# Two layers of a hybrid trunk: mLSTM normaliser states moved as rows, adaLN paced evenly with buffers of its own

## The chip, the cores and the metric

The kernel runs on one core of a Trainium2 chip. The metric is the device time of one execution in microseconds (us), median of several runs.

## The reference

Two layers work on 128 context tokens and 512 latent tokens, 640 rows of 1024 channels, in float32. Each layer computes, for either token group with its own conditioning vector:

```python
sh1, sc1, gt1, sh2, sc2, gt2 = split(silu(cvec) @ w_mod[l] + b_mod[l], 6)     # adaLN
h = rmsnorm(x, g1) * (1 + sc1) + sh1
z = h @ w_in + b_in          # inputs of four mixers and their gates
x = x + gt1 * (sum_i sigmoid(gates_i) * (mixer_i(z) @ w_b[i])) @ w_o
h = rmsnorm(x, g2) * (1 + sc2) + sh2
x = x + gt2 * (silu(h @ w1a) * (h @ w1b)) @ w2
```

Mixer A is neighbourhood attention, B dense attention with few key heads, C windowed attention with a sink, D a bidirectional mLSTM with 4 heads of 128 channels. For each head and direction D carries a matrix C (128 x 128), a normaliser n (128) and a stabiliser m. The latent tokens start from cached states (`state_C`, `state_n`, `state_m`), and the final states of the context tokens are outputs (`ml_C`, `ml_n`, `ml_m`). At the end comes one more RMSNorm.

## The kernel before

**Work and tiling.** Tokens lie in five tiles of 128 (the fifth is the context). Every matrix product is made of three fp32r matmuls per slab, for a high and a low part of both factors (`mm3`, L391 to L393). Weights come by `wload`: a DMA of 512 KB into one of two raw buffers (L374), a ScalarE cast into the high part (L379) and a VectorE subtraction for the low part (L380), into rings of five. A projection by `fm` goes over two groups of columns (256 and 384 tokens), eight slabs each, and yields after the fourth slab and at the end of each group; `tm` does the same over the five token tiles.

**Order.** `mixers` writes the order out by hand. A list of bulk work (the projections of A, D, B, C and the merges M00 to M33, each with a rate) is run by `drive`. After each yield of bulk work it calls `tick()`, and takes as many steps from the attention and mLSTM streams as the rate gives credit for. Then `layer` does the output projection (four column blocks `n`), a norm (`norm_tm`), 22 FFN columns in four groups and the next norm, with `tick()` in every yield (`run`). A scheduler then sorts the instructions of each engine by priority and a simulated time; weight loads have a high priority. All DMAs are issued by SP, in order.

**adaLN.** The modulation of a layer has 12 chunks of 512 columns (two each for shift, scale and gate of either norm). Chunks 0 to 3 of layer 0 are made in `start`. All others are background work: `bg` holds generators, and `tick()` takes `bg[0]` steps of them per tick. One step (`adaln_acc`) takes one 128 x 512 slab of `w_mod`: for the latent vector VectorE multiplies and adds it into a sum (L456); for the context vector ScalarE multiplies (L450) and GpSimd adds (L452). After eight slabs `adaln_cols` transposes both sums on TensorE (L463, four transposes into an S and four into a T bank) and reduces them on VectorE (L464). Gate chunks are transposed back, get their bias from `b_mod` and go to DRAM (`gt_d`), from where `gate_rows` loads them. Six chunks of layer 0 are queued at the first merge of C (M20), at one step per tick, and the rest is forced (`bg_steps(1000)`) before the output projection; 10, 11 and all of layer 1 follow in the FFN at 0.8 per tick. Their buffers are taken from those that attention and merges use (`qs`, `ofs`, `ta`).

**mLSTM.** `d_rows` (L1272 to L1349) makes the decay rows of all heads, with DMAs through DRAM. `d_attn` then goes over the heads: `states` loads C and n of both directions into a P buffer (L1398, L1399), `final` stores the context's C and n (L1441, L1442) from `ta`, of which there is one. Each n is a column: 128 partitions of one float, so 128 pieces of 4 bytes.

Lines of the steps below: L1571 is the last work of the merge of branch C (i = 2) of each column block, L1754 the product in an FFN column, L1595 and L1596 the residual add, L623 the front of a norm.

Of the kernel before, what the change touches and what calls it, by code (L numbers as in the profile page):

```python
# [63 lines left out]
for _i in range(4):  # L64
    for _j in range(8):
# [5 lines left out]
                           + ([np.arange(O_MI, O_MI + 16)] if h == 0 else [])) for h in range(4)]  # L71

S_N1, S_N2, S_GQ, S_GK, S_MG, S_SINK, S_BM = NFM, NFM + 8, NFM + 16, NFM + 17, NFM + 18, NFM + 22, NFM + 30
NSM = NFM + 62
# [5 lines left out]
DEFER = 2  # L80
BGRATES = (1.0, 0.8)
BGFL, BGJ, W3 = 0, 2, 1
RATES = (0.9, 0.7, 1.1, 1.1)
# [135 lines left out]
def trunk(ctx: ExitStack, tc: tile.TileContext, a: dict, depth: int):  # L219
# [84 lines left out]


    small = arena("sa", {1: 16, 2: 16, 5: 4, 10: 4, 40: 2})
    ssq = arena("ss", {1: 16})
# [157 lines left out]

    def adaln_chunk(l, ch):
        gate = (ch // 2) % 3 == 2
        accs = [ofs.take() for _ in range(2)]
        slots = [(qs, qs.take()), (ofs, ofs.take()), (ofs, ofs.take())]
        bufs = [slots[0][1][:, 0:512], slots[0][1][:, 512:1024], slots[1][1][:, :512]]  # L470
        tmps = [slots[2][1][:, :512], ta512()]

        def load(k):
            if k < KT:
                SY.dma_start(bufs[k % 3], a["w_mod"][l, P * k:P * k + P, 512 * ch:512 * ch + 512])
            elif gate and k == KT:
                for v in range(2):
                    SY.dma_start(bufs[2][4 * v:4 * v + 4, :P],
                                 a["b_mod"][l, 512 * ch:512 * ch + 512].rearrange("(j n) -> j n", n=P))

        for k in range(2):
            load(k)
        yield True
        for k in range(KT):
            adaln_acc(accs, bufs[k % 3], k, tmps[k % 2])
            load(k + 2)
            yield True
        if gate:
            col = smallb(10)[:, :8]
            adaln_cols(lambda v: col[:, 4 * v:4 * v + 4], accs)  # L490
            yield True
            ps = acc()
            T.transpose(ps[:8, :P], col, ident)
            V.tensor_tensor(bufs[0][0:8, :P], ps[:8, :P], bufs[2][0:8, :P], ALU.add)
            for v in range(2):
                SY.dma_start(gt_d[l][ch // 6, v, 512 * (ch % 2):512 * (ch % 2) + 512].rearrange("(j n) -> j n", n=P),
                             bufs[0][4 * v:4 * v + 4, :P])
        else:
            adaln_cols(lambda v: mod_slice(ch)[:, :, v], accs)
        have.add((l, ch))  # L500
        ofs.give(*accs)
        for pl, t in slots:
            pl.give(t)
        yield True

# [3 lines left out]
    def start():  # L509
# [81 lines left out]
        bigs.give(big)  # L591
        ms.give(*xT)
        return first

# [199 lines left out]
    def a_proj(l, p, d, big=None, hook=None, first=None):  # L794
# [83 lines left out]
        if first:  # L878
            SY.dma_start(tab, a["rope"])
            SY.dma_start(cmask, a["cmask"])  # L880
            SY.dma_start(bone, a["bone"])

    def a_attn(l, d):
# [375 lines left out]
    def d_rows(l, d):  # L1259
# [4 lines left out]
        ws_ = held[1][:, :NTOK]  # L1264
        rows4 = [t[:, :1280].rearrange("p (w n) -> p w n", w=2) for t in held[2:4]]
        z = zif
        lf = small(40).rearrange("p (t c) -> p t c", t=NTT)
# [9 lines left out]
        for (t0, nt) in ((0, 4), (4, 1)):  # L1277
            ps = bT()
            for tt in range(nt):
                T.transpose(ps[:16, tt * P:(tt + 1) * P], z[:, t0 + tt, :], ident)  # L1280
            S.copy(t16[:16, t0 * P:(t0 + nt) * P], ps[:16, :nt * P])
        yield
        for dr in range(2):
# [94 lines left out]
    def d_attn(l, d):  # L1378
        need = {0: (0, 1, 2, 4), 1: (3, 2, 1, 4)}

        def head(h):
# [12 lines left out]
            def states():  # L1394

                CS = st["CS"] = [p640()[:, :516].rearrange("p (c x) -> p c x", c=4) for _ in range(2)]
                for dr, c in ((0, 0), (1, 3)):
                    SY.dma_start(CS[dr][:, c, :P], a["state_C"][l, dr, h])  # L1398
                    SY.dma_start(CS[dr][:, c, P:P + 1], a["state_n"][l, dr, h].rearrange("(p o) -> p o", o=1))  # L1399

# [34 lines left out]
            def final():  # L1435
                cf = ta512()
                for dr in range(2):
                    ps = bS()
                    T.matmul(ps[:, :129], st["kws"][dr][:, 3, :], va[:, 4, :], start=True, stop=True)
                    S.copy(cf[:, 256 * dr:256 * dr + 129], ps[:, :129])  # L1440
                    SY.dma_start(a["ml_C"][l, dr, h], cf[:, 256 * dr:256 * dr + 128])  # L1441
                    SY.dma_start(a["ml_n"][l, dr, h].rearrange("(p o) -> p o", o=1),  # L1442
                                 cf[:, 256 * dr + 128:256 * dr + 129])

# [54 lines left out]
        for h in range(4):  # L1499
# [39 lines left out]
            yield  # L1539
        yield  # L1540
        yield
        heads[3][8]()
# [35 lines left out]

    have = set()

    def gate_rows(l, w):

        assert {(l, 6 * w + 4), (l, 6 * w + 5)} <= have
        gts = [p640() for _ in range(4)]
# [72 lines left out]
    def mixers(l, d, *start):  # L1657
        done.clear()

        def mg(i, jj, needs=(), rate=0.0):  # L1660
            def gen():
                if i == 2 and jj == 0 and l == 0:
                    bg[0] = BGRATES[0]
                    bg[2] += [adaln_chunk(0, ch) for ch in range(4, 10)]
                yield from merge(l, i, jj, d, i == 0, i == 2)
            return f"M{i}{jj}", needs, rate, gen()
# [26 lines left out]
    def layer(l, *start):  # L1693
# [10 lines left out]
        for n in range(2):  # L1704
            if n == BGFL:
                bg_steps(1000)
            p = wo(n)
# [6 lines left out]
            residual_tm(xs, p, KT, mg_lhs, gts, n)  # L1714
        pieces = {2: wo(2), **pieces}
        hook = norm_tm(xs, pieces, KT, mg_lhs, gts, ms, 1)
        ms.give(*extra[0])
# [3 lines left out]
        if l + 1 < depth:  # L1721
            smalls(l + 1)
        bg[0] = 0.0
        if l == 0:
            bg[2] += [adaln_chunk(0, ch) for ch in (10, 11)]
        if l + 1 < depth:
            bg[2] += [adaln_chunk(l + 1, ch) for ch in range(12)]
        j0 = 0
        for g, cnt in enumerate(FF_SPLIT):
# [4 lines left out]
            for jx in range(cnt):  # L1734
# [6 lines left out]
                if g == 3 and jx == 2:  # L1741
                    pieces[3] = fo(3, bufs)
                if j == BGJ:
                    bg[0] = BGRATES[1]
                pl = ks if g % 2 == 0 else (ms if jx < 4 else qs)
# [21 lines left out]
            if g == 3:  # L1767
                bg_steps(1000)
                if l + 1 == depth:
                    fin.append(ks.take())  # L1770
# [13 lines left out]
            j0 += cnt  # L1784
        bg[0] = 0.0
        if l + 1 < depth:
# [19 lines left out]
def layouts(x_prompt, x_sample, cache_na_kv, cache_gqa_kv, cache_swa_kv, state_mlstm_C, state_mlstm_n, state_mlstm_m,  # L1806
# [17 lines left out]
    ins["w_mod"] = f(w_mod)  # L1824
    ins["b_mod"] = f(b_mod)
    ins["wflat"] = pack_weights(w_in, f(w_branch), f(w_out), f(w_ffn_in), f(w_ffn_out))
# [10 lines left out]
    for w in range(2):  # L1837
        for s in range(2):
            at = S_BM + 16 * w + 8 * s
            sm[:, :, at:at + 8] = bm[:, 3 * w + s].transpose(0, 2, 1)  # L1840
    ins["smalls"] = sm
    ins["gqa_k_g"] = f(gqa_k_g)
    ins["btm0"] = f(b_in[:, TM0_COLS])
# [18 lines left out]
def build(ins, L):  # L1862
    import concourse.bacc as bacc

    nc = bacc.Bacc("TRN2", target_bir_lowering=False, num_devices=1)
    a = {}
# [17 lines left out]
```

## Time and profile before

| | |
|---|---|
| median of 3 runs | 2850.89 us (2850.05 to 2851.22) |
| the profiled execution | 2846.38 us, span 2844.6 us |
| TensorE busy (matmuls) | 2741.0 us, 96% |
| VectorE, ScalarE, GpSimd busy | 1870.2, 1347.7, 531.1 us |
| mean granted TensorE clock | 0.988 |

Busy time is the time in which an engine runs an instruction. In the rows below PE is TensorE's matmuls, PEld its weight loads, DVE VectorE, ACT ScalarE, POOL GpSimd, SP the engine that issues DMAs. PEclk is the granted share of TensorE's full clock. A wait `A <- B` says that A's engine stood idle until B was done.

### The profile page before, as it was taken

The numbers are of one execution on the slowest core, as the hardware profiler recorded it, in microseconds if no ns is written. First come the engines' busy times: TensorE is split into PE (matmuls) and PEld (weight loads), VectorE is DVE, ScalarE is ACT, GpSimd is POOL, SyncE is SP. The second block draws the span as 40 slices with busy tenths as digits, with TensorE's granted clock in tenths as the row PEclk, the third lists the DMA queues.
The fourth block names the chain that finished last, engine by engine and source line by source line (L and its number), as shares of the span: only waits on it lengthen the run. The fifth ranks groups of instructions, "written<-read, shape, count | busy, mean of one in ns | idle before, by whom it ended". The sixth has DMA issues, their size and how long they took to land.

```text
span 2844.6 us, 51810 instructions
## 1 busy us (share of the span) xinstructions
PE 2741.0 (96%) x19942; PEld 2692.0 (95%) x19942; DVE 1870.2 (66%) x4392; ACT 1347.7 (47%) x3122; POOL 531.1 (19%) x474
## 2 busy tenths in 40 slices
PE   8999999999988898989999999999999999999998
PEld 5999999999988898989999999999999999999998
DVE  7776567878788769785456766577888435334344
ACT  6764345656553544443237753356566334222322
POOL 0000001101166337471120000011100121101011
PEclk9999999999999999999999999999999999999999
DMA  6223331111255245452222223321111232222231
GB/s 243 83 90 92 72 69 60 46 57 60 72 164 174 94 149 160 141 164 97 90 96 81 96 92 87 63 70 45 47 62 46 90 134 68 67 82 75 72 101 66
DMA packets 117736, 264.30 MB, mean 93 GB/s; under 512 B 17536, under 2 KB 43520, under 8 KB 117488
## 3 DMA queue, kind: packets, MB, share of 16 engines
q1 hardware_dynamic: 117488, 260.99, 29.4%
q8 instruction: 156, 2.56, 0.4%
q14 instruction: 92, 0.75, 0.1%
HBM read 252.74 MB, written 7.95 MB: 92 GB/s over the span
## 4 chain that ended last, share of the span: by engine, by line
PE 75%; DVE 7%; DMA 6%; ACT 4%; issue 4%; POOL 2%; SPq 0%; DVEq 0%; POOLq 0%; ACTq 0%
PE acc L392 21%; PE acc L391 21%; PE acc L393 21%; PE O L1197 2%; DMA q<-w_mod 2%; PE T L1187 2%; DVE of L456 2%; DMA raw<-wflat 2%; DVE wlo L380 1%; DMA of<-w_mod 1%; POOL of L452 1%; ACT whi L379 1%; PE S L1154 1%; PE S L1155 1%; PE T L923 1%
## 5 line engine op out<-in xcount | busy, mean ns | idle before, releaser
L391 PE MATMUL acc<-hT,whi 128*128 128x256 f32 (+1 forms) x3392 | 1057.4, 313 | 10.2 <-DVE hT L643 3.1
L392 PE MATMUL acc<-hT,whi 128*128 128x256 f32 (+1 forms) x3392 | 1056.1, 312 | 3.3 <-DVE hT L588 1.5
L393 PE MATMUL acc<-hT,wlo 128*128 128x256 f32 (+1 forms) x3392 | 1053.5, 311 | 1.3 <-DVE wlo L380 1.3
L380 DVE TENSOR_TENSOR wlo<-raw,whi 128x512 fp32r<-128x512 f32 (+1 forms) x632 | 482.6, 768 | 398.8 <-ACT whi L379 397.0
L379 ACT CAST whi<-raw 128x512 fp32r<-128x512 f32 (+1 forms) x632 | 387.9, 619 | 630.0 <-PE acc L392 373.0
L391 PEld LDWEIGHTS acc<-hT,whi 128*128 128x128 f32 x3392 | 642.5, 190 | 16.1 <-DVE hT L643 4.1
L392 PEld LDWEIGHTS acc<-hT,whi 128*128 128x128 f32 x3392 | 643.1, 190 | 6.8 <-DVE hT L644 2.2
L393 PEld LDWEIGHTS acc<-hT,wlo 128*128 128x128 f32 x3392 | 642.6, 190 | 3.0 <-DVE wlo L380 1.8
L1596 POOL TENSOR_TENSOR big<-big,t 128x256 f32<-128x256 f32 x150 | 127.4, 852 | 603.9 <-DVE t L1595 592.1
L1566 POOL TENSOR_TENSOR m<-m,f 128x256 f32<-128x256 f32 x96 | 100.5, 1050 | 568.1 <-DVE f L1564 315.0
L391 PE MATMUL acc<-whi,kv 128*128 128x256 f32 x660 | 185.0, 283 | 7.2 <-DVE t L1595 4.4
L392 PE MATMUL acc<-wlo,kv 128*128 128x256 f32 x660 | 184.6, 283 | 3.0 <-DVE wlo L380 3.0
L393 PE MATMUL acc<-whi,kv 128*128 128x256 f32 x660 | 184.3, 282 | 0.0
L703 ACT CAST pth<-T 128x512 fp32r<-128x512 f32 (+1 forms) x232 | 118.1, 521 | 100.7 <-PE T L1187 50.1
L391 PE MATMUL acc<-big,whi 128*128 128x256 f32 (+1 forms) x512 | 158.8, 311 | 2.7 <-ACT f L1558 2.7
L393 PE MATMUL acc<-big,wlo 128*128 128x256 f32 (+1 forms) x512 | 159.9, 312 | 0.2 <-DVE wlo L380 0.2
L392 PE MATMUL acc<-big,whi 128*128 128x256 f32 (+1 forms) x512 | 158.4, 310 | 0.0
L704 DVE TENSOR_TENSOR ptl<-T,pth 128x512 fp32r<-128x512 f32 (+1 forms) x232 | 137.2, 602 | 30.2 <-ACT pth L703 29.4
L1595 DVE TENSOR_TENSOR t<-acc,P 128x256 f32<-128x256 f32 x200 | 83.2, 420 | 109.5 <-PE acc L393 97.4
L452 POOL TENSOR_TENSOR of<-of,ta 128x512 f32<-128x512 f32 x80 | 126.1, 1577 | 114.7 <-ACT of L450 91.8
L391 PEld LDWEIGHTS acc<-whi,kv 128*128 128x128 f32 x660 | 125.0, 190 | 8.3 <-DVE t L1595 5.0
L392 PEld LDWEIGHTS acc<-wlo,kv 128*128 128x128 f32 x660 | 124.1, 189 | 3.8 <-DVE wlo L380 3.8
(392 smaller groups left out, 5560.1 us busy)
## 6 DMA issues: line engine op xcount, KB each, us to landing
raw<-wflat SPq DMA_DIRECT2D x308, 512.0 KB
q<-w_mod SPq DMA_DIRECT2D x126, 256.0 KB
of<-w_mod SPq DMA_DIRECT2D x40, 256.0 KB
kv<-nbias SPq DMA_DIRECT2D x16, 576.0 KB
raw<-wflat SPq DMA_DIRECT2D x24, 256.0 KB
kv<-mdr SPq DMA_DIRECT2D x16, 320.0 KB
big<-x_sample SPq DMA_DIRECT2D x8, 512.0 KB
P<-gt_d SPq DMA_DIRECT2D x32, 128.0 KB
```

The source lines that it names most:

```text
L379: S.copy(hi[:, :n], raw[:, s0:s0 + n])
L380: V.tensor_tensor(lo[:, :n], raw[:, s0:s0 + n], hi[:, :n].bitcast(F32), ALU.subtract)
L391: T.matmul(ps, lhs(k, 0), rhs(k, 0), start=(k == 0), stop=False)
L392: T.matmul(ps, lhs(k, 0), rhs(k, 1), start=False, stop=False)
L393: T.matmul(ps, lhs(k, 1), rhs(k, 0), start=False, stop=(k == kn - 1))
L452: G.tensor_tensor(accs[v][:, :512], accs[v][:, :512], tmp, ALU.add)
L456: V.scalar_tensor_tensor(accs[v][:, :512], w, s, accs[v][:, :512], ALU.mult, ALU.add)
L703: S.copy(hi[:, :n], ps[:, :n])
L704: V.tensor_tensor(lo[:, :n], ps[:, :n], hi[:, :n].bitcast(F32), ALU.subtract)
L1566: G.tensor_tensor(mt[:, c0:c0 + n], mt[:, c0:c0 + n], gate[:, c0:c0 + n], ALU.add)
L1595: V.tensor_tensor(t[:, :256], ps[:, :256], gt[:, 256 * v:256 * v + 256], ALU.mult)
L1596: (V if n == 3 else G).tensor_tensor(xs[tt][:, 256 * n:256 * n + 256], xs[tt][:, 256 * n:256 * n + 256], t[:, :256], ALU.add)
```

## The change

The column loads and stores of n become one load and one store of 8 rows of 128 floats per layer, with a TensorE transpose each and small column copies on GpSimd (`ncol`). The background adaLN becomes one generator over all 20 chunks, started at the end of `start` and stepped at 0.25 per tick throughout, with four slab buffers, a pair of sums and one temporary of its own; between the last slab and the transposes it has two empty steps. `bg_until` makes further steps where a chunk is wanted that isn't there yet. The gate's bias comes from a constant that is loaded once. The new buffers are allocated first, in 15 KB per partition that a smaller DMA descriptor memory sets free (`dynamic_dma_scratch_size` 1024), with a pad that leaves every other buffer at its address.

```diff
-BGRATES = (1.0, 0.8)
-BGFL, BGJ, W3 = 0, 2, 1
+BGRATE = 0.25
+W3 = 1
...
+    ncol = [cp.tile([P, 8], F32, name=f"ncol{i}") for i in range(2)]
+    wm_tiles = [cp.tile([P, 512], F32, name=f"wm{i}") for i in range(4)]
+    msum = [cp.tile([P, 512], F32, name=f"msum{v}") for v in range(2)]
+    mtmp = cp.tile([P, 512], F32, name="mtmp")
+    gcol = cp.tile([P, 8], F32, name="gcol")
+    grow = cp.tile([8, P], F32, name="grow")
+    bgate = cp.tile([P, depth, 2, KT], F32, name="bgate")
+    cp.tile([P, 72], F32, name="pad")
...
-    def adaln_chunk(l, ch):
...
+    def adaln_all(items):
+        def load(x):
+            if x < KT * len(items):
+                (l, ch), k = items[x // KT], x % KT
+                SY.dma_start(wm_tiles[x % 4], a["w_mod"][l, P * k:P * k + P, 512 * ch:512 * ch + 512])
+        load(0)
+        load(1)
+        for i, (l, ch) in enumerate(items):
+            for k in range(KT):
+                adaln_acc(msum, wm_tiles[(KT * i + k) % 4], k, mtmp)
+                load(KT * i + k + 2)
+                yield True
+            yield True
+            yield True
+            if (ch // 2) % 3 == 2:
+                adaln_cols(lambda v: gcol[:, 4 * v:4 * v + 4], msum)
...
+                yield True
+                ps = acc()
+                T.transpose(ps[:8, :P], gcol, ident)
+                V.tensor_copy(grow, ps[:8, :P])
...
+            else:
+                adaln_cols(lambda v: mod_slice(ch)[:, :, v], msum)
+            have.add((l, ch))
             yield True
...
+    def bg_until(l, *chs):
+        while not all((l, ch) in have for ch in chs):
+            assert bg[2]
+            bg_steps(1)
...
+        bg[0] = BGRATE
+        bg[2].append(adaln_all([(l, ch) for l in range(depth) for ch in range(0 if l else 4, 12)]))
         return first
...
+            SY.dma_start(bgate.rearrange("p l w k -> p (l w k)"), a["bgate"])
...
+        nrow = held[1][:8, NTOK:NTOK + P]
+        SY.dma_start(nrow, a["state_n"][l].rearrange("d h p -> (d h) p"))
...
+        ps = bT()
+        T.transpose(ps[:, :8], nrow, ident[:8, :8])
+        V.tensor_copy(ncol[0], ps[:, :8])
         yield
...
-                    SY.dma_start(CS[dr][:, c, P:P + 1], a["state_n"][l, dr, h].rearrange("(p o) -> p o", o=1))
+                    G.tensor_copy(CS[dr][:, c, P:P + 1], ncol[0][:, 4 * dr + h:4 * dr + h + 1])
...
-                    SY.dma_start(a["ml_n"][l, dr, h].rearrange("(p o) -> p o", o=1),
-                                 cf[:, 256 * dr + 128:256 * dr + 129])
+                    G.tensor_copy(ncol[1][:, 4 * dr + h:4 * dr + h + 1], cf[:, 256 * dr + 128:256 * dr + 129])
...
+        ps = bT()
+        T.transpose(ps[:8, :P], ncol[1], ident)
+        nout = ta512()[:8, :P]
+        V.tensor_copy(nout, ps[:8, :P])
+        SY.dma_start(a["ml_n"][l].rearrange("d h p -> (d h) p"), nout)
...
-        assert {(l, 6 * w + 4), (l, 6 * w + 5)} <= have
+        bg_until(l, 6 * w + 4, 6 * w + 5)
...
-            if n == BGFL:
-                bg_steps(1000)
...
+        bg_until(l, *range(6, 10))
...
-                if j == BGJ:
-                    bg[0] = BGRATES[1]
...
-                bg_steps(1000)
+                if l + 1 < depth:
+                    bg_until(l + 1, *range(4))
...
-    nc = bacc.Bacc("TRN2", target_bir_lowering=False, num_devices=1)
+    nc = bacc.Bacc("TRN2", target_bir_lowering=False, num_devices=1, dynamic_dma_scratch_size=DMA_RING)
```

## Rows read from the trace of the kernel before

**Rows 1.** The page, part 1: busy us of each engine, its share, instructions.

```profile
PE 2741.0 (96%) x19942; PEld 2692.0 (95%) x19942; DVE 1870.2 (66%) x4392; ACT 1347.7 (47%) x3122; POOL 531.1 (19%) x474
```

**Rows 2.** Lines L1571 and L1754 by stretch: duration ns, first and last start us.

```profile
L1571 ACT ACTIVATE kv<-m x6: 721/737/738, 795.7 to 861.4; 128x640 fp32r<-128x640 f32 x6
...
L1571 ACT ACTIVATE kv<-m x6: 738/740/741, 2241.6 to 2293.6; 128x640 fp32r<-128x640 f32 x6
...
L1754 DVE TENSOR_TENSOR f<-acc,f x22: 409/484/558, 1200.9 to 1451.7; 128x256 f32<-128x256 f32 x11, 128x384 f32<-128x384 f32 x11
...
L1754 DVE TENSOR_TENSOR f<-acc,f x20: 423/488/558, 2635.2 to 2806.6; 128x256 f32<-128x256 f32 x10, 128x384 f32<-128x384 f32 x10
```

**Rows 3.** Busy us by stage: length, PE, PEld, DVE, ACT, POOL, PEclk, DMA, GB/s.

```profile
795.70:1451.70 656.00, 601.98 (x4342) 589.88 (x4341) 462.90 (x635) 265.69 (x488) 295.82 (x221) 0.98 0.42 133
2241.60:2806.60 565.00, 564.58 (x4200) 563.82 (x4199) 228.31 (x418) 169.46 (x334) 73.23 (x84) 1.00 0.26 84
...
800.00:900.00 100.00, 88.48 (x598) 85.42 (x598) 81.29 (x93) 45.59 (x75) 62.33 (x46) 0.97 0.54 174
```

**Rows 4.** Waits of PE, 795 to 1310 us: us in total, times, longest.

```profile
PE S L463 <- DVE of L456: 17.9, 8, 3.6
PE T L463 <- POOL of L452: 6.8, 5, 2.3
```

**Rows 5.** The chain that ended last: start us, us, what.

```profile
286.61 10.98 DMA raw<-wflat
...
402.16 9.96 DMA raw<-wflat
...
1737.16 11.22 DMA raw<-wflat
...
1851.42 9.87 DMA raw<-wflat
```

**Rows 6.** Timeline of PE from 845.8 us: start us, us, what.

```profile
845.86 0.66 PE L463 MATMUL S<-ident,of 128*128 128x128 f32 x4
846.27 0.42 PE L392 MATMUL acc<-hT,whi 128*128 128x384 f32 x1
```

**Rows 7.** VectorE by form, 100 to 200 and 800 to 900 us; then line L456.

```profile
L380 DVE TENSOR_TENSOR wlo<-raw,whi 128x512 fp32r<-128x512 f32 x16 | 10.9, 688 | 4.4 <-ACT whi L379 4.4
...
L380 DVE TENSOR_TENSOR wlo<-raw,whi 128x512 fp32r<-128x512 f32 x21 | 24.3, 1166 | 2.7 <-ACT whi L379 2.7
...
L456 DVE SCALAR_TENSOR_TENSOR of<-kv,csil,of x12: 730/732/747, 18.5 to 30.5; 128x512 f32<-128x512 f32 x12
```

**Rows 8.** Lines L452 and L464: duration ns min/median/max, first and last start us.

```profile
L452 POOL TENSOR_TENSOR of<-of,ta x80: 1263/1619/2236, 783.2 to 1305.6; 128x512 f32<-128x512 f32 x80
...
L464 DVE TENSOR_REDUCE modr<-S x12: 674/681/692, 847.4 to 1259.9; 128x4 f32<-128x512 f32 x12
```

**Rows 9.** Busy us by stage: the mixers of layer 0.

```profile
60.00:785.00 725.00, 711.87 (x5212) 704.87 (x5211) 526.87 (x1534) 415.60 (x1040) 55.12 (x50) 0.99 0.25 71
```

**Rows 10.** Busy us by stage: the two fullest windows of VectorE in those mixers.

```profile
680.00:700.00 20.00, 20.00 (x147) 19.88 (x146) 19.63 (x53) 13.39 (x34) 2.15 (x2) 1.00 0.26 80
720.00:740.00 20.00, 20.00 (x148) 19.83 (x147) 19.00 (x54) 13.57 (x34) 2.07 (x2) 1.00 0.27 89
```

**Rows 11.** DMA, 275 to 305 us in 40 slices of 0.75 us.

```profile
GB/s 87 1 0 0 0 0 0 0 0 0 0 0 105 1 4 98 17 104 0 11 27 49 27 49 38 33 38 44 324 423 368 131 0 0 0 0 0 0 0 0
```

**Rows 12.** Timeline of SP, 270 to 305 us.

```profile
286.17 0.33 SPq L1442 DMA_DIRECT2D ml_n<-ta  x1
```

**Rows 13.** Busy us by stage: the four stretches with a late weight load.

```profile
286.00:302.00 16.00, 10.04 (x71) 9.65 (x70) 5.68 (x17) 4.26 (x12) 0.00 (x0) 0.79 0.55 84
...
400.00:416.00 16.00, 12.24 (x93) 11.95 (x93) 7.42 (x24) 7.24 (x27) 1.42 (x2) 0.96 0.63 76
...
1732.00:1752.00 20.00, 16.18 (x124) 15.86 (x123) 6.89 (x17) 6.73 (x17) 0.00 (x0) 0.93 0.40 70
...
1849.00:1866.00 17.00, 13.32 (x97) 13.04 (x96) 8.42 (x25) 7.49 (x27) 1.42 (x2) 0.88 0.58 73
```

More of the change, by code (lines that the diff above doesn't have):

```diff
@@ L71 @@
                            + ([np.arange(O_MI, O_MI + 16)] if h == 0 else [])) for h in range(4)]
+DMA_RING = 1024
 S_N1, S_N2, S_GQ, S_GK, S_MG, S_SINK, S_BM = NFM, NFM + 8, NFM + 16, NFM + 17, NFM + 18, NFM + 22, NFM + 30
@@ L464, in adaln_cols @@
             V.tensor_reduce(dst(v), ps.rearrange("p (j n) -> p j n", j=4), AX.X, ALU.add)
-    def adaln_chunk(l, ch):
[L467 to L476, printed above, removed]
-                for v in range(2):
[L478 to L486, printed above, removed]
-            yield True
[L488 to L504, printed above, removed]
@@ new lines, in trunk @@
+    have = set()
+    def adaln_all(items):
[14 more added lines that the diff above has]
+                adaln_cols(lambda v: gcol[:, 4 * v:4 * v + 4], msum)
+                w, h = ch // 6, ch % 2
+                for v in range(2):
+                    V.tensor_tensor(gcol[:, 4 * v:4 * v + 4], gcol[:, 4 * v:4 * v + 4], bgate[:, l, w, 4 * h:4 * h + 4],
+                                    ALU.add)
+                yield True
+                ps = acc()
+                T.transpose(ps[:8, :P], gcol, ident)
+                V.tensor_copy(grow, ps[:8, :P])
+                for v in range(2):
+                    SY.dma_start(gt_d[l][w, v, 512 * h:512 * h + 512].rearrange("(j n) -> j n", n=P), grow[4 * v:4 * v + 4])
+            else:
+                adaln_cols(lambda v: mod_slice(ch)[:, :, v], msum)
+            have.add((l, ch))
+            yield True
@@ L1577, in merge @@
             bigs.give(d["big"])
-    have = set()
     def gate_rows(l, w):
-        assert {(l, 6 * w + 4), (l, 6 * w + 5)} <= have
+        bg_until(l, 6 * w + 4, 6 * w + 5)
         gts = [p640() for _ in range(4)]
@@ L1661, in gen @@
             def gen():
-                if i == 2 and jj == 0 and l == 0:
-                    bg[0] = BGRATES[0]
-                    bg[2] += [adaln_chunk(0, ch) for ch in range(4, 10)]
                 yield from merge(l, i, jj, d, i == 0, i == 2)
@@ L1722, in layer @@
             smalls(l + 1)
[L1723 to L1727, printed above, removed]
         j0 = 0
@@ L1767, in layer @@
             if g == 3:
-                bg_steps(1000)
-                if l + 1 == depth:
+                if l + 1 < depth:
+                    bg_until(l + 1, *range(4))
+                else:
                     fin.append(ks.take())
@@ L1784, in layer @@
             j0 += cnt
-        bg[0] = 0.0
         if l + 1 < depth:
@@ L1824, in layouts @@
     ins["w_mod"] = f(w_mod)
-    ins["b_mod"] = f(b_mod)
     ins["wflat"] = pack_weights(w_in, f(w_branch), f(w_out), f(w_ffn_in), f(w_ffn_out))
@@ L1841, in layouts @@
     ins["smalls"] = sm
+    ins["bgate"] = np.ascontiguousarray(bm[:, 2::3].transpose(3, 0, 1, 2).reshape(P, L * 2 * KT))
     ins["gqa_k_g"] = f(gqa_k_g)
```

## The prediction

> **What bounds the kernel now.** I read the page first, to see which engine is full: TensorE is busy in 2741.0 of 2844.6 us [rows 1], so nothing but its 104 us of idle time, and time at a low clock, is there to be won. Next the windows by stage, to see where those us lie. The adaLN burst of the kernel before runs from the first merge of branch C in layer 0 into that layer's FFN. Layer 1 does the same merges, output projection and FFN without adaLN, so it measures what the burst costs. From the first L1571 to the last L1754 layer 0 takes 795.7 to 1451.7 = 656.0 us, layer 1 2241.6 to 2806.6 = 565.0 us [rows 2]: 91.0 us more. In layer 0 TensorE idles 656.0 - 602.0 = 54.0 us of it at a granted clock of 0.98, in layer 1 0.4 us at 1.00 [rows 3]. The waits of TensorE there, to see what came last: the adaLN transposes L463 waited 17.9 us for VectorE's accumulation and 6.8 us for GpSimd's [rows 4]; the rest are small waits of bulk matmuls for evictions and weight splits on a crowded VectorE. Last the chain of waits in the mixers, where four stretches are no TensorE work but a weight load of 9.9 to 11.2 us [rows 5].
>
> **Part one, adaLN paced at 0.25.** It removes the burst. What stays is TensorE's own work: 20 chunks x 8 transposes; four take 846.27 - 845.86 = 0.41 us of the queue [rows 6], so 160 take 16.4 us, wherever they stand, and the eight gate transposes under 1 us. Stalls that can go: 91.0 - 17 = 74 us. Check: 54 us idle, and 2% of 656 us is 13 us at a lower clock, 67 us; the other 7 are slower matmuls inside busy time.
>
> Where the work goes. A tick is one yield of bulk work. By the code a group of 8 slabs gives two ticks, a group of 4 one: in the mixers 4 x 12 (A) + 4 x 18 (D) + 10 + 16 (B) + 8 + 16 (C) + 16 x 12 (merges) = 362, after them 20 + 20 + 22 x 8 + 120 + 20 = 356, so 718 per layer. The new generator has 8 accumulating steps per chunk, two empty ones and one or two to finish, 11 or 12: 12 plain chunks x 11 + 8 gate chunks x 12 = 228 steps, 912 ticks. So 90 steps fall in layer 0's mixers, 89 in the stretch of the old burst, 49 in the first half of layer 1's mixers: 139 of 228 move beside attention, some 97 accumulations and 12 chunk ends. Deadlines are met far ahead: the gates of chunks 4 and 5 are 24 steps = 96 ticks, wanted at tick 362, so the new forced steps cost nothing. Empty steps put over 8 ticks between the last accumulation and its transposes, which covers L463's wait.
>
> What it costs there. On VectorE an accumulation takes 0.73 us by itself; and ops that read two SBUF tensors slow down beside GpSimd's add: L380 takes 0.688 us in a stretch without adds and 1.166 us in the burst [rows 7]. GpSimd was busy in 62 of those 100 us [rows 3], so a fully covered op takes about twice as long, and a 1.6 us add [rows 8] costs VectorE at most 0.8 us: 0.73 to 1.5 us per accumulation, I take 1.2; and 1.36 us of reduces per chunk [rows 8]. With 725 us for some 350 ticks, 20 us hold 2.4 steps, 1.7 accumulations: 2.0 + 0.3 = 2.3 us more VectorE work per 20 us. Layer 0's mixers have it 526.9 of 725.0 us busy [rows 9], so the sum fits, but two windows of 20 us stand at 19.63 and 19.00 us, with TensorE full all the same [rows 10]. They overflow by 1.9 and 1.3 us, and other windows have room. Bounds for the loss in the mixers: nothing (the windows after absorb it) to the 97 x 1.5 + 24 x 0.68 = 162 us of all this work on the path. Nearest is the row in which VectorE at 98% costs TensorE nothing, so I take the two overflows with as much again for the lower clock behind a stall, 6 us; 5 us for 24 reduces that now hold a score or transpose bank between attention blocks; and 4 us for the two row chains of the mLSTM (d_rows), of many small VectorE ops, that have adaLN ops among them. A gain is excluded, since the mixers only get work. In the stretch of the old burst, where layer 1 leaves VectorE over half free [rows 3], the steps are hidden; in the two norms, where GpSimd lies on the chain, I allow 7 us. Losses: 22 us, 0 to 162. The w_mod loads (256 KB every 12 us or so) are requested two steps, about 16 us, ahead; the 9.9 to 11.2 us of the slowest loads [rows 5] lie inside that. What is queued behind one that is late is all of VectorE. A weight load that stands behind one on SP lands later by 256 KB at some 400 GB/s [rows 11], 0.7 us, and has a second raw buffer as cover. ScalarE gets one multiplication per step and is busy for 415.6 of 725 us [rows 9]; GpSimd, at 55.1 of 725 us, lets a power for a head norm wait up to 1.6 us behind an add, which the 5 and 4 us hold. The gate bias joins a load at the start instead of 16 small ones; the pad and the smaller descriptor memory have no instruction: nothing.
>
> **Part two, the normaliser states as rows.** Removed are 16 loads and 16 stores of 128 single floats each. In the stretch of the first such pair of stores the DMA moves 11 to 49 GB/s in nine slices of 0.75 us, then 324 to 423 [rows 11]; the second store is issued at 286.17 us [rows 12], and the weight load behind it at 286.61 takes 10.98 us [rows 5]. The same stands behind the stores of the last head and again in layer 1. TensorE's idle time in those four stretches is 5.96 + 3.76 + 3.82 + 3.68 = 17.2 us, and granted clocks of 0.79, 0.96, 0.93 and 0.88 lose 3.4 + 0.6 + 1.4 + 2.0 = 7.4 us [rows 13]: 24.6 us. A weight load without this takes the 11 us less those seven, 4 us, and seven is more than the longest idle time, so all 24.6 goes; the bounds are 0 (the 64 KB stores of C, which stay, are the cause) and 24.6. Added: per layer one row load, two 8-row transposes (0.1 us each by rows 6), two copies, one store, and 16 column copies on GpSimd, on a queue far from full. A transpose may wait for the row load behind a blocked SP queue: 0 to 3 us per layer, hidden by its two yields, I take 0.
>
> **Sum.** 2846.4 us (the profiled execution; its span is 2844.6) - 74 - 24.6 + 22 = 2769.8. The median of the runs is 4.5 us above that execution: 2774 us. A measurement of this kernel can tell 0.2%, 5.7 us, from no change.
>
> **Rivals.**
> - *Each step costs the same wherever it stands.* If the price is contention per accumulation and not crowding, the 74 us move along (0.46 us per accumulation of 160) and only the state part counts: 2850.9 - 24.6 = 2826. For it: the slowing of L380 is per add. Against: a third of the 74 us are transposes that followed their sums too closely [rows 4], and VectorE is at 527 of 725 us in the mixers.
> - *The late weight loads stay late*, because the C stores or the queue's order cause them: 2774 + 24.6 = 2799. Against: the slow stretch moves too few bytes for its time.
> - *Slower: VectorE becomes the bound of layer 0's mixers.* The place is the score, maximum, normalise, transpose chain of branches B and C, 460 to 780 us, and A in layer 1; the price is up to 162 us of new VectorE work, against 98.6 us won. It decides once over 61% of it shows on TensorE; with 80%, 2850.9 - 98.6 + 130 = 2882. For it: windows at 98% and 95%. Against: TensorE is full in these very windows. A rule of the Trainium skill speaks for it: the page GPSIMD Engine Reference, section Specifications, says that GpSimd shares its SBUF interfaces with VectorE, with contention for VectorE instructions of two SBUF inputs. If an add stopped such instructions for its whole 1.6 us, 97 adds would block up to 155 us. The trace agrees with the rule only in part: L380 slows by 0.48 us in the burst and is not stopped.
> - The new pace not being kept would need the forced steps, which by the count above never come; its chance lies in the mixtures below.
>
> **How the numbers follow.** My forecast (losses of 0 to 45 us: 2752 to 2797) 0.62; late loads stay 0.10; price moves along 0.14; VectorE bound 0.07; mixtures around no change 0.07. The range runs from 2755 to 2815: the forecast, the late loads, and mixtures of it with the unchanged price. Faster by over 0.2%: 0.62 + 0.10 + 0.14 + 0.03 = 0.89; within 0.2% 0.04; slower 0.07.
>
> **What would show it.** In the profile after, 795 to 1310 us loses its idle slices, L463 no longer leads TensorE's waits, and the stretch from first L1571 to last L1754 of layer 0 is under 585 us. Right for part two: no 10 us load in the chain, and the four stretches full at clock 1.00. Wrong: TensorE idle behind VectorE between 460 and 780 us or in 1500 to 1900, VectorE waiting for w_mod, or L1345 or L463 late in the mixers.

## The result, and the profile after

The changed kernel takes 2798.59 us (median of 4 runs, 2795.42 to 2801.26) beside 2850.47 us of the kernel before in the same session (2849.51 to 2851.22): a ratio of 0.9824, 95% interval 0.9811 to 0.9836. It is 51.9 us faster, where the sum had said 76.6. The profiled execution has a span of 2796.0 us.

The page of the kernel after, part 1, against [rows 1]; TensorE is at 98% now.

```profile
PE 2727.5 (98%) x19946; PEld 2679.6 (96%) x19946; DVE 1853.6 (66%) x4412; ACT 1352.5 (48%) x3122; POOL 520.4 (19%) x506
```

Busy time by stage, columns as in [rows 3]: from the first merge of C to the last FFN product, layer 0 and layer 1; then the mixers of layer 0 (from the first key eviction of A) and everything from the last FFN product of layer 0 to the merges of layer 1.

```profile
816.80:1394.70 577.90, 572.81 (x4254) 571.13 (x4253) 326.03 (x518) 213.07 (x402) 163.80 (x144) 1.00 0.35 112
2193.30:2758.20 564.90, 564.48 (x4200) 563.72 (x4199) 228.38 (x417) 169.43 (x334) 73.46 (x84) 1.00 0.25 84
...
61.00:816.80 755.80, 738.26 (x5376) 724.27 (x5375) 606.81 (x1635) 458.11 (x1113) 126.70 (x115) 1.00 0.28 87
1394.70:2193.30 798.60, 777.70 (x5702) 768.29 (x5701) 621.23 (x1687) 469.13 (x1165) 124.08 (x124) 0.99 0.25 81
```

The stretch of the old burst went from 656.0 to 577.9 us, with 5.1 us of idle TensorE where there were 54.0. But the mixers now have 17.5 and 20.9 us of idle TensorE, 38.4 together, beside a VectorE that is busy in about 80% of the time. The same two stretches in state_only, the kernel before with the states as rows (see below), which has no adaLN there, hold 3.3 and 8.0 us, 11.3 together:

```profile
54.80:783.80 729.00, 725.74 (x5332) 719.01 (x5330) 542.15 (x1555) 427.00 (x1066) 65.50 (x72) 1.00 0.23 73
1442.20:2219.00 776.80, 768.76 (x5660) 761.27 (x5660) 573.56 (x1639) 448.59 (x1134) 84.36 (x96) 1.00 0.23 74
```

Waits of TensorE from 816.8 to 1331.1 us, against [rows 4]: us in total, times, longest. The adaLN transposes (L478 now) are gone from the list.

```profile
PE acc L406 <- DVE t L1623: 3.2, 3, 1.3
PE acc L407 <- POOL hT L662: 1.2, 1, 1.2
PE acc L406 <- DVE hT L661: 0.6, 1, 0.6
```

The weight loads among the rows of the chain that ended last, against [rows 5] (start us, us). None of about 10 us is left; the longest takes 5.43 us.

```profile
254.14 5.43 DMA raw<-wflat
...
317.46 4.21 DMA raw<-wflat
...
438.19 3.36 DMA raw<-wflat
...
1455.09 3.22 DMA raw<-wflat
...
1664.61 5.13 DMA raw<-wflat
```

Spans of all profiled kernels, in us, cut at the same three marks of each trace: the first L1571 (L1601 after) of layer 0, the last L1754 (L1771) of layer 0, and the first L1571 of layer 1 (the same statements in the other kernels). The experiments below refer to it. "Ratio" is against the kernel before in the same session. In the session of state_only, adaln_only, paced and late_start one of thirteen executions of the kernel before took 4492.3 us at a granted clock of 0.562; it is left out here, which makes that kernel's median there 2848.9 us.

| kernel | to the merges of C, layer 0 | merges, output, FFN, layer 0 | to the merges of C, layer 1 | rest | span | VectorE busy | ratio (interval) |
|---|---|---|---|---|---|---|---|
| before | 795.7 | 656.0 | 789.9 | 603.0 | 2844.6 | 1870.2 | 1 |
| after | 816.8 | 577.9 | 798.6 | 602.7 | 2796.0 | 1853.6 | 0.9824 (0.9811, 0.9836) |
| state_only | 783.8 | 658.4 | 776.8 | 602.8 | 2821.8 | 1872.4 | 0.9891 (0.9870, 0.9913) |
| adaln_only | 836.6 | 579.4 | 831.8 | 602.9 | 2850.7 | 1850.0 | 0.9975 (0.9958, 0.9991) |
| paced | 815.0 | 581.0 | 795.4 | 602.7 | 2794.1 | 1821.7 | 0.9800 (0.9783, 0.9816) |
| late_start | 815.6 | 577.7 | 802.7 | 602.7 | 2798.7 | 1853.5 | 0.9809 (0.9791, 0.9828) |
| no_acc | 794.7 | 572.1 | 783.4 | 602.9 | 2753.1 | 1662.4 | 0.9668 (0.9648, 0.9687) |
| no_cols | 822.8 | 610.9 | 777.7 | 602.7 | 2814.1 | 1836.8 | 0.9882 (0.9862, 0.9902) |
| placed | 819.0 | 598.5 | 775.7 | 602.7 | 2795.9 | 1859.3 | 0.9834 (0.9818, 0.9851) |
| placed_paced | 792.8 | 594.3 | 775.5 | 602.7 | 2765.3 | 1836.6 | 0.9719 (0.9704, 0.9733) |
| no_v0 | 797.8 | 572.8 | 787.3 | 603.8 | 2761.7 | 1719.2 | 0.9718 (0.9702, 0.9734) |
| no_v1 | 796.3 | 570.8 | 785.3 | 603.0 | 2755.4 | 1755.5 | 0.9696 (0.9682, 0.9711) |
| pp_even | 789.2 | 582.5 | 788.8 | 602.7 | 2763.2 | 1821.4 | 0.9729 (0.9715, 0.9744) |
| pp_dve | 796.3 | 586.6 | 777.1 | 602.7 | 2762.7 | 1861.2 | 0.9715 (0.9700, 0.9729) |

Against state_only, which differs from it by part one alone, the kernel after wins 80.5 us in the second column and gives 33.0 and 21.8 us back in the first and third. About 10 us of these 54.8 are TensorE's own transposes, moved there (12 chunks at 0.82 us); some 45 us are stalls: 27 us more idle time in the rows above, 6.2 us of a later start (61.0 against 54.8), and 12 us in which TensorE is busy for longer. The row of adaln_only is some 12 us too long to compare: its profiled execution was the slowest of ten (2852.49 us, median 2840.28).

### The profile page after: what moved, and what is told of

Same layout as the page of the kernel before. It is cut to its first block, busy times and chain, and to the rows that moved or that the text cites. A ratio compares the mean times of both kernels' runs of the same rounds, so it can differ in the third digit from the quotient of the medians.

```text
span 2796.0 us, 51577 instructions
## 1 busy us (share of the span) xinstructions
PE 2727.5 (98%) x19946; PEld 2679.6 (96%) x19946; DVE 1853.6 (66%) x4412; ACT 1352.5 (48%) x3122; POOL 520.4 (19%) x506
## 4 chain that ended last, share of the span: by engine, by line
PE 82%; DVE 9%; ACT 3%; issue 2%; DMA 2%; POOL 1%; SPq 0%; DVEq 0%; POOLq 0%; ACTq 0%
PE acc L406 23%; PE acc L407 23%; PE acc L408 23%; PE O L1216 2%; PE T L1206 2%; DVE msum L471 2%; DVE wlo L395 1%; DMA raw<-wflat 1%; PE S L1173 1%; DMA wm<-w_mod 1%; PE S L1174 1%; PE T L942 1%; ACT whi L394 1%; PE S L1473 0%; PE S L1182 0%
## 5 line engine op out<-in xcount | busy, mean ns | idle before, releaser
L395 DVE TENSOR_TENSOR wlo<-raw,whi 128x512 fp32r<-128x512 f32 (+1 forms) x632 | 475.7, 757 | 366.0 <-ACT whi L394 363.6
L467 POOL TENSOR_TENSOR msum<-msum,mtmp 128x512 f32<-128x512 f32 x140 | 206.6, 1476 | 387.3 <-ACT msum L465 269.9
L465 ACT ACTIVATE mtmp<-wm,csil 128x512 f32<-128x512 f32 x140 | 101.1, 722 | 121.8 <-POOL msum L467 109.1
L471 DVE SCALAR_TENSOR_TENSOR msum<-wm,csil,msum 128x512 f32<-128x512 f32 x140 | 148.2, 1059 | 7.4 <-DMA wm<-w_mod 6.2
```

What stands on the lines that cost most here:

```text
L395: V.tensor_tensor(lo[:, :n], raw[:, s0:s0 + n], hi[:, :n].bitcast(F32), ALU.subtract)
L465: S.activation(accs[v][:, :512] if kk == 0 else tmp, w, AF.Copy, scale=s)
L467: G.tensor_tensor(accs[v][:, :512], accs[v][:, :512], tmp, ALU.add)
L471: V.scalar_tensor_tensor(accs[v][:, :512], w, s, accs[v][:, :512], ALU.mult, ALU.add)
```

## The experiments

**The two parts alone.** state_only is the kernel before with the states as rows (with the smaller descriptor memory and a pad, so that all other buffers stay where they were); adaln_only is the kernel after with the states as columns. The edit of adaln_only, without its loss of the row load, the row store and their transposes:

```diff
-                    G.tensor_copy(CS[dr][:, c, P:P + 1], ncol[0][:, 4 * dr + h:4 * dr + h + 1])
+                    SY.dma_start(CS[dr][:, c, P:P + 1], a["state_n"][l, dr, h].rearrange("(p o) -> p o", o=1))
...
-                    G.tensor_copy(ncol[1][:, 4 * dr + h:4 * dr + h + 1], cf[:, 256 * dr + 128:256 * dr + 129])
+                    SY.dma_start(a["ml_n"][l, dr, h].rearrange("(p o) -> p o", o=1),
+                                 cf[:, 256 * dr + 128:256 * dr + 129])
```

> The kernel before with the normaliser states as rows alone; adaLN as before, all other buffers at their addresses. Theory (the one-float stores make four weight loads late): those loads land within 5 us, the four stretches fill, and the time falls by the 24.6 us of the prediction, to about 2826. Rival (the loads are late for the order of the queue or the C stores): a load of some 10 us stays in the chain and the time stays at 2845 to 2851.

> The changed kernel with the states as columns again, so the adaLN part alone. Theory (the two parts add up): 2798.6 + 24.6 = about 2823, with the late loads back in the chain. Rival (the adaLN work in the mixers covers what the states cost, or the two parts overlap): under 2812.

state_only took 2822.39 us, 26.5 us under the kernel before (by ratio 31, interval 25 to 37), as its theory said. The rows of its chain hold one weight load, and a short one:

```profile
1160.74 3.23 DMA raw<-wflat
```

The stores of C stay. Of the first and the last head of each layer, where the late loads had been, they are issued at 283, 392, 1724 and 1831 us, and TensorE is full around all four (276 to 302, 390 to 416, 1700 to 1740 and 1820 to 1860 us) at a granted clock of 1.00. So the stores of C were not the cause.

adaln_only took 2840.28 us (10 runs, 2835.2 to 2852.49), only 8.7 us under the kernel before (by ratio 7, interval 3 to 12); theory and rival had both expected less time. So the parts don't add: 26.5 + 8.7 = 35.2, against 51.9 for both. With steps of adaLN in the mixers, the one-float stores delay `w_mod` slabs as they delayed weights, and then it is VectorE that stands still, with everything queued behind that sum. Two rows of the chain of adaln_only (start us, us), then its waits from 1583 to 1891 us, where layer 1's heads are:

```profile
1803.06 8.98 DMA ml_n<-ta
1812.46 11.15 DMA wm<-w_mod
```

```profile
PE S L1469 <- DVE kv L1479: 16.2, 2, 11.1
...
DVE msum L471 <- DMA wm<-w_mod: 12.2, 2, 9.6
```

Part one needs part two.

**Is the new pace kept?** It isn't. The adds of GpSimd in the kernel after (L467, one per step), in windows of 20 us: busy us, count, granted clock, DMA.

```profile
260.00:280.00 20.00, 0.00 (x0) 1.00 0.32 101
280.00:300.00 20.00, 4.35 (x3) 1.00 0.24 68
300.00:320.00 20.00, 6.27 (x5) 1.00 0.48 144
320.00:340.00 20.00, 0.00 (x0) 1.00 0.43 129
340.00:360.00 20.00, 0.00 (x0) 1.00 0.24 79
360.00:380.00 20.00, 5.97 (x5) 1.00 0.31 90
```

An even pace has 1.5 adds in each (1.7 accumulations, of which the first of each eight needs no add). A step depends on its load, on the sum before it and on the transposes that free `msum`; nothing ties it to the bulk work at whose yield it was issued. So the scheduler, which sorts by priority and simulated time, draws a chunk's steps together. It did the same at the start: SP had issued eleven slab loads before A's first key eviction at 61.0 us (start us, us).

```profile
31.28 2.37 SPq L489 DMA_DIRECT2D wm<-w_mod  x4
...
41.93 5.61 SPq L489 DMA_DIRECT2D wm<-w_mod  x4
...
54.35 6.93 SPq L489 DMA_DIRECT2D wm<-w_mod  x3
```

In state_only that eviction comes at 54.8 us. In paced each instruction of an accumulation is tied, without a semaphore, behind the instruction that precedes it on its engine in the order of the program; late_start begins the background work at the first projection of D.

```diff
+        if tmp is not None:
+            held, at = {}, len(nc.cur_bb.bb.instructions)
+            for ins in nc.cur_bb.bb.instructions[::-1]:
+                held.setdefault(str(ins.engine), ins)
...
+            for ins in nc.cur_bb.bb.instructions[at:]:
+                if str(ins.engine) in held:
+                    after(ins, held[str(ins.engine)], "steps in the order of the trace")
```

```diff
-        bg[0] = BGRATE
...
+        if l == 0 and h == 0:
+            bg[0] = BGRATE
```

> The changed kernel; each accumulation of the background adaLN is tied, on its own engine, behind the instruction that stands before it in the order of the program, so the scheduler can't draw a chunk's eight steps together. Theory (the shortfall against the forecast, some 30 us, comes from chunks that run as bursts of eight accumulations in 16 to 25 us): the bursts are gone, ScalarE hardly waits for GpSimd's adds any more, and the time falls by 15 to 35 us, to 2764 to 2784. Rival (the work itself costs its time on VectorE and GpSimd, however it is spaced): 2793 to 2803.

> The changed kernel with the background adaLN begun at the first projection of D, 48 ticks later, still at 0.25. Theory (twelve slab loads and eight accumulations drawn into the start cost 7 us there, and the next chunk costs some of A's 12 us): first key evacuation of A back from 61.0 to about 54 us, time down by 7 to 15 us, to 2784 to 2792. Rival (the loss at the start returns later, where the work goes): 2796 to 2802.

Both theories missed, and both times lie in the range of the rival. paced took 2795.45 us and late_start 2797.96. In paced the start is back at 54.7 us, but TensorE idles in the mixers as before:

```profile
54.70:815.00 760.30, 738.94 (x5361) 726.81 (x5360) 602.15 (x1632) 455.44 (x1113) 129.98 (x116) 0.99 0.28 87
1396.00:2191.40 795.40, 777.73 (x5702) 766.27 (x5701) 621.38 (x1692) 470.37 (x1169) 129.19 (x129) 1.00 0.26 83
```

That is 21.4 and 17.7 us, 39.0 together, against 38.4 after. The ties do spread the adds, to two or three in most windows of 20 us, but with mixed success: between the first query eviction of B and the merges of layer 0 paced is 7.1 us shorter than the kernel after, between the first key eviction of A and that point it is 11.6 us longer, for a reason that was not looked for. So spacing by ties alone wins little on the whole, and this run doesn't tell how much of the cost is bunching. In late_start the start stayed at 61.9 us: the scheduler drew the first steps forward past the new starting point too (its first add stands at 41.0 us).

**Accumulations or transposes?** Theory A: the sums cost it; theory B: the transposes and reduces, which hold a bank. no_acc leaves out the sums (a copy of one column waits for each slab), no_cols the transposes and reduces (two copies of 128 x 4 take their place).

```diff
-                adaln_acc(msum, wm_tiles[(KT * i + k) % 4], k, mtmp)
+                V.tensor_copy(msum[0][:, k:k + 1], wm_tiles[(KT * i + k) % 4][:, :1])
```

```diff
-                adaln_cols(lambda v: mod_slice(ch)[:, :, v], msum)
+                adaln_skip(lambda v: mod_slice(ch)[:, :, v], msum)
```

> The changed kernel without the accumulations of the background adaLN: the slabs are loaded, one float per partition of each is copied into the sum, transposes and reduces stay (left out: the modulation values of all chunks but the first four). Theory A (VectorE's and GpSimd's accumulations cost the mixers their 45 us): stages of the mixers as in the run with the states alone, up to 3.5 us of transposes each, time near 2750. Theory B (transposes and reduces in the S and T banks cost it): 2785 to 2798. Theory C (the slab loads in SP's order cost it): 2785 to 2798, with no_cols no lower than its TensorE work explains.

> The changed kernel without the transposes and reduces of the background adaLN; loads and accumulations stay, two copies of four columns stand for each chunk's end (left out: the sum over the partitions, so the modulation values). Theory B: besides the 17 us of TensorE's own work the stalls of the mixers go, time near 2745 to 2755. Theory A: only the 17 us and part of the reduces go, 2772 to 2785.

no_acc took 2753.68 us, 45 us under the kernel after, as A said; it keeps the slab loads, so C is out. Its mixers (first and third column) are 22.1 and 15.2 us shorter, its second column 5.8. So of the 45 us of stalls in the mixers the sums hold 37, and some 8 stay in no_acc, with its transposes, reduces and loads. The kernel after has 82 of its 140 adds in the mixers and the other 58 in the merges, output projection and FFN: for each add a step costs (22.1 + 15.2) / 82 = 0.45 us in the mixers, the start included, and 5.8 / 58 = 0.1 us beside merges and FFN (0.40 and 0.09 us per accumulation). no_cols has less work than the kernel after and took 2814.73 us, 16 us more, which neither theory had. The loss is in the second column (610.9 us). There no_cols has 84 adds, and none are left for the third; 36 of them stand between 840 and 980 us, where the kernel after has 13. At that pace the work is dear beside merges and FFN too: the column is 38.8 us longer than that of no_acc, some 0.5 us per add. It seems that the transposes were also what kept the scheduler from drawing one chunk's sums on to the next. That reading was not tried by itself.

**Which half of a step?** In no_v0 VectorE's sum keeps only its first slab; in no_v1 the other sum does, so that GpSimd's adds and ScalarE's products go.

```diff
-            else:
+            elif tmp is None:
                 V.scalar_tensor_tensor(accs[v][:, :512], w, s, accs[v][:, :512], ALU.mult, ALU.add)
```

```diff
-                S.activation(accs[v][:, :512] if kk == 0 else tmp, w, AF.Copy, scale=s)
-                if kk:
-                    G.tensor_tensor(accs[v][:, :512], accs[v][:, :512], tmp, ALU.add)
+                if kk == 0:
+                    S.activation(accs[v][:, :512], w, AF.Copy, scale=s)
```

> The kernel after, but the sums of the first time vector keep only their first slab (seven of eight VectorE accumulations per chunk are left out, so that vector's modulation is not the reference's); ScalarE's products, GpSimd's adds, loads and transposes stay. Leaving out all accumulations took 45 us. If it is VectorE's own time that costs it (V), most of that goes here: about 2760 to 2770 us. If it is GpSimd's adds and ScalarE's wait for them (G), about 10 us at most go: 2785 to 2799.

> The mirror of it: the kernel after, but the sums of the second time vector keep only their first slab, so GpSimd's adds and ScalarE's products go (seven of eight per chunk) and VectorE's accumulations stay. G expects most of the 45 us here, 2760 to 2770 us, with VectorE's accumulation faster than its 1.06 us mean in the kernel after; V expects 2785 to 2799. If both runs lose some 20 to 25 us, it is the sum of the two.

Either way most of the 45 us comes back: by ratio 30 us without VectorE's half and 36 without the other. V expected that of no_v0 alone and G of no_v1 alone, so neither half by itself is the cause; and 30 and 36 make more than 45, so either half costs less once the other is gone. The mixers of no_v1, where VectorE still does every one of its sums:

```profile
55.70:796.30 740.60, 731.58 (x5378) 722.43 (x5377) 578.13 (x1634) 429.99 (x1066) 60.35 (x67) 1.00 0.28 89
1367.10:2152.40 785.30, 773.97 (x5701) 765.73 (x5700) 599.27 (x1687) 451.41 (x1137) 83.93 (x96) 1.00 0.25 83
```

VectorE has as many instructions as in the kernel after, yet 98 us less busy time (1755.5 against 1853.6), 0.70 us for each add that went. The trace of the kernel after shows how an add costs VectorE time. Timeline of GpSimd, then of VectorE, 302 to 311 us (start, us):

```profile
303.37 2.00 POOL L467 TENSOR_TENSOR msum<-msum,mtmp 128x512 f32<-128x512 f32 x1 [0.84 <-ACT mtmp L465]
306.20 1.28 POOL L467 TENSOR_TENSOR msum<-msum,mtmp 128x512 f32<-128x512 f32 x1 [0.83 <-ACT mtmp L465]
308.32 1.29 POOL L467 TENSOR_TENSOR msum<-msum,mtmp 128x512 f32<-128x512 f32 x1 [0.83 <-ACT mtmp L465]
...
302.89 0.73 DVE L471 SCALAR_TENSOR_TENSOR msum<-wm,csil,msum 128x512 f32<-128x512 f32 x1
...
306.32 1.71 DVE L471 SCALAR_TENSOR_TENSOR msum<-wm,csil,msum 128x512 f32<-128x512 f32 x1
...
308.69 1.48 DVE L471 SCALAR_TENSOR_TENSOR msum<-wm,csil,msum 128x512 f32<-128x512 f32 x1
```

The sum of 302.89 began with GpSimd idle and took 0.73 us. That of 306.32 began 0.12 us into an add and ended at 308.03, 0.55 us after the add's end at 307.48. That of 308.69 ended at 310.17, 0.56 us after the add's end at 309.61. Both stood still until the add was done. It goes the other way too: the add of 303.37, which began during VectorE's work, took 2.00 us in place of 1.28. Over all 140 the spread fits that (min, median and max in ns): 1842 is one whole add and 0.55 us.

```profile
L471 DVE SCALAR_TENSOR_TENSOR msum<-wm,csil,msum x140: 729/752/1842, 40.4 to 1780.0; 128x512 f32<-128x512 f32 x140
```

The Trainium skill, page SBUF — State Buffer, section Summary: rules for kernel authors, says so: beside a VectorE instruction with two SBUF inputs, a GpSimd instruction that reads SBUF blocks or is blocked, the later one waiting for the whole of the other. This trace agrees at each of these places.

**Where to put the work.** placed starts the generator at the first projection of B, with a rate of 0.3 in the mixers and 0.55 in the FFN, so that all is done before layer 1; placed_paced has the ties as well.

```diff
-BGRATE = 0.25
+BGRATES = (0.3, 0.55)
...
+        if l == 0:
+            bg[0] = BGRATES[0]
...
+        bg[0] = BGRATES[1]
```

> The changed kernel with the background adaLN begun at the projection of B in layer 0, at 0.3 per tick, and at 0.55 from the FFN of layer 0 on, so that all 20 chunks end before layer 1; nothing of it lies in the start, in A and D, or in layer 1. Theory (A and D, the start and layer 1 cost 44 us of the 55 us that the work adds outside the old burst; the FFN takes a chunk for some 1.7 us): 2755 to 2772, the stretch from the first L1571 to the last L1754 of layer 0 at some 590 us. Rival (crowding again: the FFN at twice the pace stalls as the old burst did): 2785 to 2800.

> The same with each accumulation tied behind the instruction before it on its engine. Theory (tying made branches B and C cheaper by 7 us in the run paced, and cost A and D 11 us, which have no adaLN here): 5 to 8 us below placed. Rival: within 3 us of it.

placed took 2801.04 us, no better than the kernel after; placed_paced 2767.52 us (2766.92 to 2771.2), 31 us better than it and the fastest up to here that leaves nothing out. The expected sizes were wrong: the tie was to be worth 5 to 8 us, and it is worth 33. Line L471 of placed, then the same line (L477) of placed_paced, first and last start:

```profile
L471 DVE SCALAR_TENSOR_TENSOR msum<-wm,csil,msum x140: 726/752/1880, 42.8 to 1361.3; 128x512 f32<-128x512 f32 x140
```

```profile
L477 DVE SCALAR_TENSOR_TENSOR msum<-wm,csil,msum x140: 729/746/1868, 388.8 to 1346.7; 128x512 f32<-128x512 f32 x140
```

Without the tie the scheduler drew the first chunk forward by some 350 us, to the start; with it the program's place holds, with 30 adds left in layer 0's mixers, 110 in the merges and FFN, and none in layer 1's mixers. But that is not where the 26.2 us between the two first columns lie. placed has only 35 adds in its first column, and both kernels reach the first key eviction of C at nearly the same time (602.0 and 600.5 us); from there to the merges placed takes 217.0 us and placed_paced 192.3. In placed seven adds, a chunk's transposes and the writing out of a gate chunk fall together there. Its row from 610 to 640 us shows VectorE full, TensorE idle for 11.2 us, and a granted clock of 0.66:

```profile
610.00:640.00 30.00, 18.80 (x78) 15.97 (x78) 29.71 (x52) 16.21 (x35) 11.62 (x8) 0.66 0.29 90
```

So most of what the tie is worth lies where a burst of adaLN met a full VectorE. In placed_paced the 30 adds make the first column 9.0 us longer than that of state_only, some 3 of them transposes: 0.2 us for each add.

**Rate and engine, in the best version.** pp_even is placed_paced at 0.38 throughout; pp_dve does both sums on VectorE:

```diff
-            if v and tmp is not None:
+            if v and kk == 0 and tmp is not None:
```

> The placed and tied kernel (2767.5 us) with one rate of 0.38 from the first projection of branch B to the end of the feed-forward part, in place of 0.3 and then 0.55. If the price of a tied step is the same anywhere from B on, it stays at 2765 to 2770 us. If a step in the mixers costs more than one in the merges and the feed-forward part, it gets slower, by up to 0.08 x 242 ticks = 19 steps at some 0.3 us: 2773 us, all of it between the first query eviction of B and the first merge.

> The placed and tied kernel (2767.5 us) with both sums on VectorE (GpSimd's 140 adds and ScalarE's 140 products go, 140 more accumulations on VectorE come). If contention with GpSimd's adds is what its remaining 30 us or so of stalls are made of, it gets faster, 2755 to 2765 us; if it is VectorE's occupancy, slower: 2770 to 2785 us.

pp_even took 2768.52 us and pp_dve 2764.13, beside 2845.54 for the kernel before in that session. By their ratios neither differs from placed_paced. pp_even's total is as expected for an equal price, but its stages are not: it wins 11.8 us in the second column and loses 13.3 in the third, where 14 of its adds now stand and placed_paced has none. pp_dve lies at the upper end of the range for contention (2755 to 2765), but no clear step below placed_paced, so it decides for neither. Its line of sums (busy us, mean ns of one):

```profile
L477 DVE SCALAR_TENSOR_TENSOR msum<-wm,csil,msum 128x512 f32<-128x512 f32 x280 | 218.0, 816 | 3.0 <-ACT msum L471 2.8
```

140 more sums of 0.816 us are 114 us for VectorE, but its busy time grew by only 24.6 us (1836.6 to 1861.2). So an add on GpSimd had cost VectorE (114 - 24.6) / 140 = 0.64 us, nearly as much as doing it there.

## Why the prediction was right, and where it was not

**The direction, and the bound.** Right. TensorE's idle time and its lower clock were all there was to win, and the burst held most of it. The stretch was to fall under 585 us and is at 577.9; TensorE's waits for the transposes are gone. That the time falls inside the range is in part luck: 2798.59 us lies just above the forecast's own band (2752 to 2797), and the range went on to 2815 for late loads and an unchanged price, neither of which came.

**Part two.** Right: 24.6 us forecast, 26.5 measured alone, the 10 us loads left the chain, and TensorE is full around the stores of C. The rival *late loads stay* happens to give the measured total (2799 us), and is wrong all the same: a total doesn't name its cause. What it missed is the coupling that adaln_only shows.

**The 74 us of stalls.** Right in size. Against state_only the second column falls by 80.5 us, of which 10 are transposes that moved; with the 5.8 us that its sums still cost there, 76 us of stalls went.

**The losses of 22 us.** Here it failed, and this is the whole shortfall: some 45 us of stalls in the start and the mixers and 6 in the second column, in place of 15 for the mixers and 7 for the norms. That is 29 us more, of which the other two terms gave back some 4. Of the 45 us the sums hold 37 (no_acc), forecast at 6 and 4; the 8 beside them stand against 5 for reduces that hold a bank. Three steps failed, not equally.

- "20 us hold 2.4 steps" assumed an even pace. The trace has chunks drawn together, and steps at the start, which had been costed at nothing: the start took 6.2 us more. paced restores the start and spreads the adds, and won only 3 us, as A and D got longer for a reason that is not known; so the share of this step stays open.
- "I take the two overflows with as much again" is the term that was mis-sized. VectorE's added work was right: 1.2 us per accumulation forecast, and (1853.6 - 1662.4 + 20.1) / 160 = 1.3 between the kernel after and no_acc, whose small copies take 20.1 us in their place. What was wrong is how much of it TensorE feels. I took the window of 20 us at 98%, with TensorE full [rows 10], as nearest. A mean over 20 us does not show how long one eviction or subtraction waits behind a stalled sum, and 82 adds in the mixers cost 0.45 us each.
- The rule on GpSimd and VectorE was set aside because L380 "slows by 0.48 us in the burst and is not stopped". That 1.166 us was a mean over instructions that met an add and others that did not. The line in the kernel before, from 800 to 900 us (min, median, max in ns), holds both:

```profile
L380 DVE TENSOR_TENSOR wlo<-raw,whi x21: 676/752/1781, 799.7 to 886.4; 128x512 fp32r<-128x512 f32 x21
```

The long ones began during an add and ended some 0.55 us after it (852.00 us, 1.78 us long, beside an add from 851.84 to 853.23). The price per add (0.64 to 0.70 us of VectorE) lay inside my bound of 0.8, so the sum used nearly the right figure for the wrong reason.

**The rivals.** *VectorE becomes the bound* had the right place (layer 0's mixers and layer 1's) and the wrong share: of the 162 us some 45 show on TensorE, 28% and not over 61%. *Each step costs the same wherever it stands* had 0.46 us per accumulation, and the mixers pay 0.40, but no_acc puts it at 0.09 us beside merges and FFN, so place does matter, but not as forecast: spread beside merges and FFN a step is cheap, and it is the mixers that pay. Nor is place all: crowded as in no_cols, the steps cost some 0.5 us per add beside merges and FFN as well.

**What stays open.** Removing either half of a step brings back 30 or 36 of 45 us, so the price is not proportional to VectorE's time; where it turns was not tried. Nor was why the sums of no_cols run on, what the 14 adds of pp_even meet in its third column, nor the 22 us by which the second column of placed_paced is still longer than that of no_acc (some 6 of them are seven more chunks' transposes).

## What to carry to other kernels

Price background work by what the busiest shared engine does for its neighbours in that stage, not by whether its mean busy time has room: in the kernel after the same steps cost 0.45 us for each add in the start and beside attention, and 0.1 us beside long projections, but some 0.5 us there too where no_cols ran them nearly three times as fast. Look at where they run in the trace before trusting a rate in the source, and tie them to their place if the scheduler may move them. Take single rows, not a mean, to judge whether two engines merely slow each other or exclude each other.

## What the hardware showed that was not expected

- A VectorE instruction with two SBUF inputs does not share with GpSimd's add, it waits for the add's end (1.48 and 1.71 us in place of 0.73), and an add begun during such work stretches from 1.28 to 2.00 us. Moving an add to GpSimd saved little: placed_paced with both sums on VectorE takes the same time as with one of them on GpSimd.
- Stores of single floats delayed the load behind them on the queue, to 10 or 11 us [rows 5], and what that costs depends on who waits: 26.5 us when weights were late, and 51.9 - 8.7 = 43 us when `w_mod` slabs were late too. (The loads of single floats went with them; no run tells the two apart.) The page of state_only counts 12960 packets under 512 B, that of the kernel before 17536. The Trainium skill, page DMA: Bandwidth & Descriptors, section Specifications, gives 512 B as the least transfer for full rate; the runs agree in direction, and none varied the size.
